# The first layer's preparation with its inverses and key products on VectorE, and the attention's keys and values projected earlier

## The chip, the cores and the metric

The kernel runs on one core of a Trainium2 chip. Its time is the device time in microseconds of one execution. The core has five engines, each with an in-order queue of its own: TensorE (PE; its weight loads are listed as PEld), VectorE (DVE), ScalarE (ACT), GpSimd (POOL) and SyncE (SP), which here starts most of the DMA transfers. The granted TensorE clock is given as a share of the full 2.4 GHz.

## What is computed

The program is a trunk of two layers over 256 context tokens and 512 latent tokens of width 1024, batch 1. The even layer has global attention with normalised queries and keys beside RWKV-7 time mixing in two directions; the odd layer has windowed attention beside a Mamba-2 mixer; each has a squared-ReLU MLP, and a last RMSNorm ends it. The change lies in the preparation of the first layer's time mixing. The part of the reference that this preparation rewrites:

```python
def rwkv7_scan(state0, r, w, k, v, kk, a, reverse):
    def step(S, inp):
        r_t, w_t, k_t, v_t, kk_t, a_t = inp
        sa = jnp.einsum('bhvk,bhk->bhv', S, kk_t)
        S = (S * w_t[:, :, None, :] - sa[..., None] * (kk_t * a_t)[:, :, None, :]
             + v_t[..., None] * k_t[:, :, None, :])
        return S, jnp.einsum('bhvk,bhk->bhv', S, r_t)
...
    kk = (k * k_k).astype(F32).reshape(bsz, T, B_HEADS, HEAD_DIM)
    kk = kk * lax.rsqrt(jnp.sum(kk * kk, axis=-1, keepdims=True) + 1e-12)
    k_dir = k.astype(F32)[:, :, None] * (1.0 + (a - 1.0) * k_a.astype(F32))
```

The kernel does the recurrence in chunks of 32 tokens. For that it needs, for each chunk, head and direction, the inverse of a unit triangular 32x32 matrix made of products of the decayed keys.

## The kernel before, in words

The program is written with a tile scheduler: the source gives the instructions with priorities (`tc.high_priority()`, and `tc.high_priority(-400)` for work that may wait), and the scheduler turns them into one fixed queue for each engine. The order of a queue is thus settled before the program runs, and an instruction that waits holds back everything behind it on its engine.

The stage of interest is in `tile_trunk` and takes from about 100 to 365 us. 768 tokens stand along the free axis, 128 channels (two heads) on the partitions, so the eight heads of the time mixing are four pairs, p = 0 to 3. For each pair the loop does the following:

- `rates(p)`: two small products on TensorE (`lora`, L653) and their tanh on ScalarE (L665).
- `body(p, d)` for both directions d: `kd` on ScalarE (L711) and its product with the keys on GpSimd (L712); `aa` on VectorE (L714); the cumulative sum of the decays on VectorE (L718); the exponentials `e` and `ei` on ScalarE (L723, L724; `ei` has one buffer); the two `ar` products on VectorE (L733, L734); the two `kb` products, one on GpSimd (L735) and one on VectorE (L736); and two transfers that write `ar` and `kb` to memory (L737, L739).
- `load_k`, `load_r` and `load_v` of the next pair: projections on TensorE (L367, three matmuls for each block of weights, since weights and activations are split in two parts, L279 and L280), the token shift on VectorE (L612) and for the keys a norm (sums on TensorE at L623, L381 on VectorE, a power on GpSimd at L382, broadcast at L628 and L631).
- `triangles(p)`: 96 small matmuls `ab` on TensorE (L797), evicted with a mask on VectorE into `abm` (L806). 24 chunks of a pair against 32 in one inverse: three inverses serve the four pairs, and they can begin after pairs 1, 2 and 3.
- `inverse(g)`, g = 0, 1, 2: a transpose on VectorE (L771), two memsets on GpSimd (L773, L774), then 31 pairs of instructions, a multiplication (L778) and a subtraction (L780), each needing the one before, and two transposes back (L781, L782). The results of g = 0 and 1 go to memory through `ttD`, that of g = 2 stays in the tile `lor`. g = 0 and 2 run on VectorE, g = 1 on GpSimd.
- `tail(p)`: the bonus and the gate (L746 to L760).

Behind the loop stand the projections of the attention: `aqk` (keys), `avv` (values) and four queries, each again 48 matmuls of L367, with a norm and a rotation on VectorE (L829 to L831). Then the mixing stage begins: `z` products (L981), and `u` products (L1032), which read all three inverses; their eviction is the first `vu` (L1037). The attention's scores (L1143) run between them. At the other end of the program `to_out` multiplies the normalised latent tokens (L1774) and writes them out.

Of the kernel before, what the change touches and what calls it, by code (L numbers as in the profile page):

```python
# [13 lines left out]
ALU = mybir.AluOpType  # L14
# [4 lines left out]
P = 128  # L19
# [205 lines left out]
def tile_trunk(ctx: ExitStack, tc: tile.TileContext, t: dict, out, cc: Cols, pc: Cols):  # L225
# [303 lines left out]
    with ExitStack() as sa:  # L529
# [140 lines left out]
        def ch(x):  # L670
            return x.rearrange("p (c t) -> p c t", t=C)
# [34 lines left out]
        def body(p, d, kd, mats, sg, a):  # L706

            k, kk, r = ks[p], kks[p], rs_[p]
            A.activation(out=sg, in_=sg, func=AF.Copy, scale=0.5, bias=0.5)
            kd_ = ap.tile([P, NT], F32, tag="kd", name=u("kd"), bufs=2)  # L710
            A.activation(out=kd_, in_=a, func=AF.Identity, scale=kah[:, p:p + 1], bias=kac[:, p:p + 1])  # L711
            G.tensor_tensor(out=kd_, in0=kd_, in1=k, op=ALU.mult)  # L712

# [20 lines left out]
            V.tensor_tensor(out=ar[:, :, 1, :], in0=ch(kk), in1=fa_, op=ALU.mult)  # L734
            G.tensor_tensor(out=kb[:, :, d, :], in0=ch(kd_), in1=fb_, op=ALU.mult)  # L735
            V.scalar_tensor_tensor(out=kb[:, :, 1 - d, :], in0=ch(a), scalar=0.5, in1=fb_, op0=ALU.mult, op1=ALU.mult)  # L736
# [28 lines left out]

        def inverse(g, eng):

            m = lor if g == 2 else aq.tile([P, 1024], F32, tag="im", name=u("im"), bufs=1)
            tmp = aq.tile([P, 256], F32, tag="scan" if g == 2 else "it", name=u("it"), bufs=1)
            m = m.rearrange("p (a b) -> p a b", b=32)  # L770
            V.transpose(m.rearrange("p a b -> p (a b)"), abm[g])  # L771
            n = abm[g]
            G.memset(n, 0.0)  # L773
            G.memset(n.rearrange("p a b -> p (a b)")[:, ::33], 1.0)  # L774
            for s in range(31):
                rows, w = 31 - s, s + 1
                tm = tmp[:, 0:rows * w].rearrange("p (a b) -> p a b", b=w)
                eng.tensor_tensor(out=tm, in0=m[:, s + 1:32, s:s + 1].to_broadcast([P, rows, w]),  # L778
                                in1=n[:, s:s + 1, 0:w].to_broadcast([P, rows, w]), op=ALU.mult)
                eng.tensor_tensor(out=n[:, s + 1:32, 0:w], in0=n[:, s + 1:32, 0:w], in1=tm, op=ALU.subtract)  # L780
            V.transpose(m[0:64].rearrange("p a b -> p (a b)"), n[0:64].rearrange("p a b -> p (a b)"))  # L781
            V.transpose(m[64:128].rearrange("p a b -> p (a b)"), n[64:128].rearrange("p a b -> p b a"))  # L782
            if g < 2:
                nc.sync.dma_start(ttD[g], m.rearrange("p a b -> p (a b)"))

        def triangles(p, mats):
# [22 lines left out]
            for g in range(NCH * p // 32, NCH * (p + 1) // 32):  # L809

                with (ExitStack(), tc.high_priority())[g - 1] if g else tc.high_priority(-400):
                    inverse(g, G if g == 1 else V)
        def attention_qk(n, nm, j):
# [49 lines left out]
        for p in range(4):  # L863
            kd, mats = [], []
            f = rates(p)
            body(p, 0, kd, mats, *f[0])
            if p < 3:
                load_k(p + 1)
            body(p, 1, kd, mats, *f[1])
            triangles(p, mats)  # L870
            if p < 3:
                load_r(p + 1)
            tail(p, kd)
            if p < 3:
                load_v(p + 1)
        for f in (aqk, avv, *q_):
            f()
# [864 lines left out]
    with ExitStack() as se:  # L1742
# [18 lines left out]
        def to_out(s):  # L1761
# [9 lines left out]
            for k in range(0, KT, 2):  # L1771
                xs = xl[:, k:k + 2, ts]
                eng = G if s == LATS[0] and k < 4 else V
                eng.tensor_tensor(out=xs, in0=xs, in1=bc.unsqueeze(1).to_broadcast([P, 2, s[1]]), op=ALU.mult)  # L1774
                nc.sync.dma_start(out[:, k:k + 2, ts], xs)
# [24 lines left out]
```

## Time and profile before

| | |
|---|---|
| Time, median of 3 runs | 2028.16 us (2027.13 to 2031.48) |
| The profiled execution | 2029.69 us, span 2027.9 us |
| Mean granted clock | 0.975 |
| TensorE busy | 1900.6 us, 94% |
| VectorE busy | 1217.1 us, 60% |
| ScalarE busy | 842.6 us, 42% |
| GpSimd busy | 360.6 us, 18% |

The shares are averages over the whole program. The stage of the change is 13% of it, and there the engines stand otherwise: what it is worth is read from stretches of that stage. A group of instructions gives the line, the engine, the operation, what is written and read, and a count behind x. A timeline row has the start and the length in us, and in brackets how long its engine was idle ahead of it and what released it.

### The profile page before, as it was taken

The page shows a single profiled execution, that of the slowest core. Times are in us where ns is not written, and L with a number is a line of the kernel's source. Part 1 is how long each engine was busy: PE and PEld are TensorE (multiplying, and loading weights), DVE is VectorE, ACT ScalarE, POOL GpSimd, SP SyncE. Part 2 cuts the span into 40 slices and gives each one's busy share as a digit, 9 for nine tenths or more (in the row PEclk, how much of TensorE's full clock was granted, in tenths as well). Part 3 has the DMA queues.
Part 4 walks back from the last instruction along what each step waited for, and adds up shares of the span by engine and source line. Part 5 has one row for each costly group of instructions (what it writes and reads, how often), then busy time and mean ns, then how long its engine had stood idle before and what let it go on. Part 6 is the DMA issues. An engine that isn't in the chain of part 4 may idle for free.

```text
span 2027.9 us, 34250 instructions
## 1 busy us (share of the span) xinstructions
PE 1900.6 (94%) x13992; PEld 1547.3 (76%) x13992; DVE 1217.1 (60%) x2070; ACT 842.6 (42%) x1419; POOL 360.6 (18%) x371
## 2 busy tenths in 40 slices
PE   6999868899999899999999999899899799999997
PEld 4776647776765898888888889778668487888886
DVE  5577969575677675555544443865677464344436
ACT  4344432455554443332233224554566444333335
POOL 0022276333222430000000002310153120000002
PEclk9999979899999999999999999999899799999998
DMA  9346554842323643344444432212101133323333
GB/s 333 120 146 193 195 174 143 166 98 59 90 59 110 230 124 93 115 125 135 125 126 131 128 94 73 87 45 73 42 1 43 42 95 97 100 86 102 94 99 109
DMA packets 147885, 228.19 MB, mean 113 GB/s; under 512 B 65024, under 2 KB 102288, under 8 KB 147600
## 3 DMA queue, kind: packets, MB, share of 16 engines
q1 hardware_dynamic: 140912, 213.54, 35.8%
q10 hardware_dynamic: 5456, 7.73, 1.1%
q0 software_dynamic: 1360, 4.73, 0.7%
q8 instruction: 110, 1.80, 0.4%
q14 instruction: 47, 0.39, 0.1%
HBM read 200.00 MB, written 25.96 MB: 111 GB/s over the span
## 4 chain that ended last, share of the span: by engine, by line
PE 69%; DVE 13%; DMA 7%; ACT 4%; issue 4%; POOL 3%; SPq 0%; DVEq 0%; POOLq 0%; ACTq 0%
PE m L367 37%; PE win L367 9%; PE po L341 4%; DMA wmod<-in_wmod_dram 4%; PE pt L332 3%; PE z L981 2%; DVE wlo L280 2%; PE wout L1714 2%; PE wout L1298 2%; PE sc L1143 2%; DMA wraw<-in_win_dram 1%; PE z L1556 1%; DVE junk L1315 1%; PE s L1047 1%; DVE it L778 1%
## 5 line engine op out<-in xcount | busy, mean ns | idle before, releaser
L279 ACT ACTIVATE whi<-wraw 128x1024 fp32r<-128x1024 f32 x214 | 226.4, 1059 | 691.1 <-PE m L367 555.7
L280 DVE TENSOR_TENSOR wlo<-wraw,whi 128x1024 fp32r<-128x1024 f32 x214 | 263.7, 1234 | 204.3 <-ACT whi L279 201.5
L367 PE MATMUL m<-hh,whi 128*128 128x512 f32 (+1 forms) x816 | 239.6, 345 | 3.9 <-ACT relu L1237 2.4
L367 PE MATMUL m<-hh,wlo 128*128 128x512 f32 (+1 forms) x816 | 242.1, 345 | 0.4 <-DVE wlo L280 0.4
L367 PE MATMUL m<-hl,whi 128*128 128x512 f32 (+1 forms) x816 | 241.9, 344 | 0.2 <-POOL hl L503 0.2
L367 PE MATMUL m<-dh,whi 128*128 128x256 f32 (+1 forms) x832 | 238.9, 342 | 2.7 <-DVE xl L1219 2.5
L367 PE MATMUL m<-dl,whi 128*128 128x256 f32 (+1 forms) x832 | 241.1, 341 | 0.0
L367 PE MATMUL m<-dh,wlo 128*128 128x256 f32 (+1 forms) x832 | 240.0, 342 | 0.1
L471 POOL TENSOR_TENSOR acc<-acc,nsq 128x256 f32<-128x256 f32 x42 | 43.6, 1047 | 870.9 <-ACT nsq L470 867.0
L367 PEld LDWEIGHTS m<-dh,whi 128*128 128x128 f32 x832 | 153.4, 188 | 24.9 <-DVE xl L1219 6.2
L367 PEld LDWEIGHTS m<-hh,whi 128*128 128x128 f32 x816 | 152.4, 189 | 23.6 <-ACT relu L1237 2.8
L367 PEld LDWEIGHTS m<-hh,wlo 128*128 128x128 f32 x816 | 153.7, 189 | 20.0 <-DVE wlo L280 0.9
L367 PEld LDWEIGHTS m<-hl,whi 128*128 128x128 f32 x816 | 153.8, 189 | 19.2 <-POOL hl L503 0.4
L367 PEld LDWEIGHTS m<-dl,whi 128*128 128x128 f32 x832 | 154.0, 188 | 18.9
L367 PEld LDWEIGHTS m<-dh,wlo 128*128 128x128 f32 x832 | 153.8, 188 | 18.8 <-DVE wlo L280 0.3
L367 PE MATMUL win<-hl,whi 128*128 128x512 f32 (+1 forms) x512 | 162.2, 350 | 4.7 <-POOL hl L503 3.5
L367 PE MATMUL win<-hh,whi 128*128 128x512 f32 (+1 forms) x512 | 158.0, 355 | 8.6 <-DVE kr L381 5.6
L367 PE MATMUL win<-hh,wlo 128*128 128x512 f32 (+1 forms) x512 | 160.3, 347 | 1.8 <-DVE wlo L280 1.8
L1315 DVE SCALAR_TENSOR_TENSOR junk<-wmod,crow 128x1024 f32<-128x1024 f32 x64 | 78.4, 1225 | 119.0 <-DMA wmod<-in_wmod_dram 118.4
L1219 DVE SCALAR_TENSOR_TENSOR xl<-m,modT,xl 128x512 f32<-128x512 f32 (+1 forms) x144 | 97.3, 686 | 72.2 <-PE m L367 72.2
L367 PEld LDWEIGHTS win<-hh,whi 128*128 128x128 f32 x512 | 95.4, 194 | 31.2 <-issue 12.3
L367 PEld LDWEIGHTS win<-hl,whi 128*128 128x128 f32 x512 | 98.9, 194 | 21.1 <-POOL hl L503 4.7
(416 smaller groups left out, 3624.3 us busy)
## 6 DMA issues: line engine op xcount, KB each, us to landing
wraw<-in_w_dram SPq DMA_DIRECT2D x136, 512.0 KB, 3.6
wmod<-in_wmod_dram SPq DMA_DIRECT2D x96, 512.0 KB, 4.1
wraw<-in_wout_dram SPq DMA_DIRECT2D x40, 512.0 KB, 3.7
wraw<-in_win_dram SPq DMA_DIRECT2D x35, 512.0 KB, 4.0
arD<-ar SPq DMA_DIRECT2D x8, 768.0 KB, 4.2
kbD<-kb SPq DMA_DIRECT2D x8, 768.0 KB, 3.7
ari<-arD SPq DMA_DIRECT2D x24, 256.0 KB, 4.3
kbd<-kbD SPq DMA_DIRECT2D x48, 128.0 KB, 4.0
```

The lines of the kernel that those rows point to most:

```text
L279: A.activation(out=hi, in_=src, func=AF.Copy)
L280: (lo_eng or V).tensor_tensor(out=lo, in0=src, in1=hi.bitcast(F32), op=ALU.subtract)
L332: T.transpose(pt[:, P * j:P * j + P], prob[j][:, P * m:P * m + P], ident)
L341: T.matmul(po[HALVES[i], :], lhsT=vt[:, k_, r], rhs=w_, start=m_ < 2, stop=m_ + 2 >= n, tile_position=(0, 64 * i))
L367: T.matmul(part(ps, s), lhsT=a[:, c], rhs=row(b, k, s), start=first and j == 0 and q == 0, stop=last and j == n - 1 and q == 2)
L471: (V if k == KT - 1 else eng).tensor_tensor(out=at(acc, s), in0=at(acc, s), in1=at(sq, s), op=ALU.add)
L981: T.matmul(ps[:, P * (2 * a + c):P * (2 * a + c) + P], lhsT=kb[:, 2 * m + a, c, :], rhs=ar[:, 2 * m + a, c, :], start=True, stop=True)
L1143: T.matmul(ps[:, cols2(s)], lhsT=qs[:, 2 * j + g, :], rhs=kx[:, g, s[0]:s[0] + s[1]], start=m == 0, stop=m == 1)
L1219: V.scalar_tensor_tensor(out=xs, in0=part(ps, s), scalar=mod(l, which, m, s[2]), in1=xs, op0=ALU.mult, op1=ALU.add)
L1298: T.matmul(part(ps, s), lhsT=a[:, c], rhs=like(b, s), start=k == 0 and q == 0, stop=k == KT - 1 and q == 2)
L1315: V.scalar_tensor_tensor(out=junk, in0=wm, scalar=1.0, in1=crow[:, :, v], op0=ALU.mult, op1=ALU.mult, accum_out=modT[:, l, n, v:v + 1])
L1714: T.matmul(o, lhsT=a[:, c], rhs=b, start=k == 0 and q == 0, stop=k == KT - 1 and q == 2)
```

## The change

Four things change. In `body` the `kd` product (L712) and the `kb` product (L735) go from GpSimd to VectorE, eight instructions each over the four pairs. All three inverses run on VectorE; the second now has the low priority of the first. For the last pair the attention's keys and values are written ahead of `triangles`, no longer behind the loop. In `to_out` the two products that GpSimd did for the first half of the latent tokens go to VectorE.

```diff
-            G.tensor_tensor(out=kd_, in0=kd_, in1=k, op=ALU.mult)
+            V.tensor_tensor(out=kd_, in0=kd_, in1=k, op=ALU.mult)
...
-            G.tensor_tensor(out=kb[:, :, d, :], in0=ch(kd_), in1=fb_, op=ALU.mult)
+            V.tensor_tensor(out=kb[:, :, d, :], in0=ch(kd_), in1=fb_, op=ALU.mult)
...
-        def inverse(g, eng):
+        def inverse(g):
...
-                eng.tensor_tensor(out=tm, in0=m[:, s + 1:32, s:s + 1].to_broadcast([P, rows, w]),
+                V.tensor_tensor(out=tm, in0=m[:, s + 1:32, s:s + 1].to_broadcast([P, rows, w]),
                                 in1=n[:, s:s + 1, 0:w].to_broadcast([P, rows, w]), op=ALU.mult)
-                eng.tensor_tensor(out=n[:, s + 1:32, 0:w], in0=n[:, s + 1:32, 0:w], in1=tm, op=ALU.subtract)
+                V.tensor_tensor(out=n[:, s + 1:32, 0:w], in0=n[:, s + 1:32, 0:w], in1=tm, op=ALU.subtract)
...
-                with (ExitStack(), tc.high_priority())[g - 1] if g else tc.high_priority(-400):
-                    inverse(g, G if g == 1 else V)
+                with tc.high_priority(*((-400,) if g < 2 else ())):
+                    inverse(g)
...
             body(p, 1, kd, mats, *f[1])
+            if p == 3:
+
+                aqk()
+                avv()
             triangles(p, mats)
...
-        for f in (aqk, avv, *q_):
+        for f in q_:
             f()
...
                 eng = G if s == LATS[0] and k < 4 else V
-                eng.tensor_tensor(out=xs, in0=xs, in1=bc.unsqueeze(1).to_broadcast([P, 2, s[1]]), op=ALU.mult)
+                V.tensor_tensor(out=xs, in0=xs, in1=bc.unsqueeze(1).to_broadcast([P, 2, s[1]]), op=ALU.mult)
```

Lines behind the loop stand four higher in the changed kernel (L981 is L985 there, L1037 is L1041). The queues differ at three places that matter here.

TensorE around the last triangles (`ab`). Before, they follow the small products of pair 3 at once, and a projection's rows come behind:

```order
L653 MATMUL lora_2446<-ad_668,lor 128x256
L653 MATMUL lora_2447<-ad_668,lor 128x512
L653 MATMUL lora_2448<-ad_668,lor 128x512
L797 MATMUL ab_2505<-ar_2474,kb_2475 32x32 x16
L797 MATMUL ab_2506<-ar_2474,kb_2475 32x32 x32
L797 MATMUL ab_2505<-kb_2498,ar_2497 32x32 x16
L797 MATMUL ab_2506<-kb_2498,ar_2497 32x32 x32
L750 MATMUL bonus_2675<-kd_2460,cst 128x256
L750 MATMUL bonus_2676<-kd_2460,cst 128x512
L756 MATMUL gate_2683<-gd_675,g2w 128x256
L756 MATMUL gate_2684<-gd_675,g2w 128x512
```

In the changed kernel there stand ahead of them the values' projection, a whole query and half of the next one (`win`, the last of it shown):

```order
L367 MATMUL win_2961<-hh,whi_2965 128x256
L367 MATMUL win_2961<-hl,whi_2965 128x256
L367 MATMUL win_2961<-hh,wlo_2966 128x256
L848 MATMUL vtok_2672<-cst,vraw_2668 128x128 x4
L797 MATMUL ab_2683<-ar_2474,kb_2475 32x32 x16
L797 MATMUL ab_2684<-ar_2474,kb_2475 32x32 x32
L797 MATMUL ab_2683<-kb_2498,ar_2497 32x32 x16
L797 MATMUL ab_2684<-kb_2498,ar_2497 32x32 x32
L750 MATMUL bonus_2853<-kd_2460,cst 128x256
```

The `ab` rows are the same; what stands ahead of them grew by about two projections.

VectorE ahead of the last triangles. Before, the products of pair 3 stand in one piece, without `kd` and `kb` of GpSimd:

```order
L733 TENSOR_TENSOR ar_2474<-fr_2318,e_2467 128x24x32
L734 TENSOR_TENSOR ar_2474<-kk_2046,e_2467 128x24x32
L714 SCALAR_TENSOR_TENSOR aa_2453<-aa_2453,kk_2046 128x768
L736 SCALAR_TENSOR_TENSOR kb_2475<-aa_2453,ei_2468 128x24x32
L714 SCALAR_TENSOR_TENSOR aa_2454<-aa_2454,kk_2046 128x768
L736 SCALAR_TENSOR_TENSOR kb_2498<-aa_2454,e_2490 128x24x32
L746 TENSOR_TENSOR kd_2460<-kd_2460,kd_2483 128x768
L734 TENSOR_TENSOR ar_2497<-kk_2046,ei_2491 128x24x32
L747 SCALAR_TENSOR_TENSOR kd_2460<-kd_2460,par,fr_2318 128x768
L733 TENSOR_TENSOR ar_2497<-fr_2318,ei_2491 128x24x32
```

In the changed kernel the steps of the second inverse (`abm_1654`) and rotations of the attention stand among them, and so do L712 and L735:

```order
L712 TENSOR_TENSOR kd_2460<-kd_2460,fk_2027 128x768
L714 SCALAR_TENSOR_TENSOR aa_2453<-aa_2453,kk_2046 128x768
L778 TENSOR_TENSOR it_2185<-im_2184,abm_1654 128x135
L735 TENSOR_TENSOR kb_2475<-kd_2460,ei_2468 128x24x32
L829 TENSOR_TENSOR rs_2587<-rot_2585,cst 128x512
L830 TENSOR_TENSOR qf_2569<-qf_2569,cst 128x512
L712 TENSOR_TENSOR kd_2483<-kd_2483,fk_2027 128x768
L714 SCALAR_TENSOR_TENSOR aa_2454<-aa_2454,kk_2046 128x768
L736 SCALAR_TENSOR_TENSOR kb_2475<-aa_2453,ei_2468 128x24x32
L780 TENSOR_TENSOR abm_1654<-abm_1654,it_2185 128x27x5
L381 TENSOR_SCALAR rr_2582<-qksum_2575 128x12
L831 TENSOR_TENSOR qf_2569<-qf_2569,rs_2587 128x512
```

Four products moved in for this pair, and steps of an inverse that were not on this engine before.

VectorE ahead of the first `vu`. Before, the third inverse has long ended there:

```order
L987 TENSOR_TENSOR z_3284<-z_3762,cst 128x4x64
L838 TENSOR_SCALAR sq_99<-rr_3206 128x6x2
L987 TENSOR_TENSOR zk_3778<-z_3773,cst 128x256
L987 TENSOR_TENSOR z_3285<-z_3773,cst 128x4x64
L987 TENSOR_TENSOR zk_3787<-z_3782,cst 128x256
L987 TENSOR_TENSOR z_3285<-z_3782,cst 128x4x64
L1037 SCALAR_TENSOR_TENSOR vu_3844<-u_3827,cst,vm_3271 128x256
```

In the changed kernel its last steps (`abm_2182`) and its transposes into `lor` stand right ahead of it:

```order
L778 TENSOR_TENSOR it_2783<-lor,abm_2182 128x60
L780 TENSOR_TENSOR abm_2182<-abm_2182,it_2783 128x2x30
L778 TENSOR_TENSOR it_2783<-lor,abm_2182 128x31
L991 TENSOR_TENSOR zk_3778<-z_3773,cst 128x256
L991 TENSOR_TENSOR z_3285<-z_3773,cst 128x4x64
L780 TENSOR_TENSOR abm_2182<-abm_2182,it_2783 128x31
L991 TENSOR_TENSOR zk_3787<-z_3782,cst 128x256
L991 TENSOR_TENSOR z_3285<-z_3782,cst 128x4x64
L781 STREAM_TRANSPOSE lor<-abm_2182 64x1024
L782 STREAM_TRANSPOSE lor<-abm_2182 64x1024
L1041 SCALAR_TENSOR_TENSOR vu_3844<-u_3827,cst,vm_3271 128x256
```

The third inverse now ends with the row ahead of `vu`, because the steps of the second alternate with its own.

## Rows read from the trace of the kernel before

**Rows 1.** Stretches of the stage: length, busy PE, PEld, DVE, ACT, POOL, granted clock, DMA

```profile
120.00:220.00 100.00, 97.53 (x854) 70.53 (x852) 79.18 (x121) 39.66 (x64) 25.51 (x20) 1.00 0.61 194
220.00:260.00 40.00, 33.88 (x284) 24.66 (x285) 34.60 (x54) 9.67 (x15) 10.74 (x8) 0.91 0.57 191
260.00:300.00 40.00, 23.50 (x339) 13.89 (x338) 28.36 (x31) 14.13 (x26) 31.41 (x38) 0.74 0.53 159
300.00:340.00 40.00, 34.12 (x195) 29.07 (x196) 38.61 (x69) 15.49 (x31) 32.53 (x39) 0.97 0.49 136
340.00:380.00 40.00, 33.61 (x268) 28.24 (x267) 27.58 (x54) 10.75 (x21) 17.42 (x18) 0.88 0.79 181
```

**Rows 2.** Waits from 200 to 300 us: line <- releaser, microseconds, times, longest

```profile
PE ab L797 <- DVE kb L736: 8.3, 1, 8.3
...
PE ab L797 <- DVE ar L734: 7.9, 1, 7.9
...
PE win L367 <- DVE kr L381: 5.6, 1, 5.6
```

**Rows 3.** Timeline ahead of the last triangles: start us, us, engine, line, operation

```profile
284.32 2.51 POOL L712 TENSOR_TENSOR kd<-kd,fk 128x768 f32<-128x768 f32 x1
286.79 1.66 POOL L735 TENSOR_TENSOR kb<-kd,ei 128x768 f32<-128x768 f32 x1
...
289.77 2.42 DVE L734 TENSOR_TENSOR ar<-kk,ei 128x768 f32<-128x768 f32 x1
...
292.24 2.77 PE L797 MATMUL ab<-kb,ar 64*32 64x32 f32 x96 [7.90 <-DVE ar L734]
...
294.70 1.05 DVE L806 TENSOR_TENSOR abm<-ab,cst 128x256 f32<-128x256 f32 x2
```

**Rows 4.** Single operations on the VectorE timeline of the stage

```profile
232.58 0.94 DVE L714 SCALAR_TENSOR_TENSOR aa<-aa,kk 128x768 f32<-128x768 f32 x1
233.45 0.40 DVE L780 TENSOR_TENSOR abm<-abm,it 128x247 f32<-128x247 f32 x1
233.77 0.94 DVE L736 SCALAR_TENSOR_TENSOR kb<-aa,e 128x768 f32<-128x768 f32 x1
...
245.52 0.33 DVE L778 TENSOR_TENSOR it<-im,abm 128x175 f32<-128x175 f32 x1
245.89 0.34 DVE L780 TENSOR_TENSOR abm<-abm,it 128x175 f32<-128x175 f32 x1
...
372.88 0.88 DVE L1037 SCALAR_TENSOR_TENSOR vu<-u,cst,vm 128x256 f32<-128x256 f32 x2 [2.40 <-PE u L1032]
```

**Rows 5.** Groups on GpSimd, 100 to 365 us: xcount | busy us, mean ns | idle

```profile
L778 POOL TENSOR_TENSOR it<-im,abm 128x31 f32<-128x31 f32 (+15 forms) x31 | 20.4, 659 | 2.1
L780 POOL TENSOR_TENSOR abm<-abm,it 128x31 f32<-128x31 f32 (+15 forms) x31 | 20.0, 645 | 2.1
L712 POOL TENSOR_TENSOR kd<-kd,fk 128x768 f32<-128x768 f32 x8 | 18.1, 2262 | 14.6 <-ACT kd L711 14.4
...
L735 POOL TENSOR_TENSOR kb<-kd,e 128x768 f32<-128x768 f32 x4 | 9.0, 2252 | 0.0
L735 POOL TENSOR_TENSOR kb<-kd,ei 128x768 f32<-128x768 f32 x4 | 8.4, 2110 | 0.1
```

**Rows 6.** Groups on VectorE in the same view, 100 to 365 us

```profile
L780 DVE TENSOR_TENSOR abm<-abm,it 128x31 f32<-128x31 f32 (+15 forms) x62 | 27.1, 436 | 1.5
...
L778 DVE TENSOR_TENSOR it<-lor,abm 128x31 f32<-128x31 f32 (+15 forms) x31 | 16.8, 542 | 2.1 <-POOL abm L774 1.3
L714 DVE SCALAR_TENSOR_TENSOR aa<-aa,kk 128x768 f32<-128x768 f32 x8 | 13.9, 1740 | 0.4 <-ACT kd L711 0.4
```

**Rows 7.** One stretch, instructions of L367 alone: length, busy PE, PEld, clock, DMA, GB/s

```profile
299.80:309.40 9.60, 8.87 (x48) 7.38 (x48) 1.00 0.49 117
```

**Rows 8.** Timeline of VectorE at the end of the program

```profile
2013.83 3.44 DVE L1774 TENSOR_TENSOR xl<-xl,rms 128x512 f32<-128x512 f32 x2
...
2021.48 2.48 DVE L1774 TENSOR_TENSOR xl<-xl,nbc 128x512 f32<-128x512 f32 x4 [0.68 <-PE nbc L490]
```

## The prediction

> **What bounds the kernel now.** I read the page first (TensorE is busy 94% of the span), then the stretches of 20 to 100 us for a place where it is not, then the waits inside it, the timeline around those waits, and last the groups of instructions on the two engines between which the change moves work. From 120 to 220 us TensorE is busy 97.5 of 100 us at the full 2.4 GHz, so there is nothing to win while it stays the bound. From 220 to 380 us it is idle 6.1, 16.5, 5.9 and 6.4 us per 40, which is 34.9 us, and the granted clock is 0.91, 0.74, 0.97 and 0.88 there; busy time multiplied by what is missing from 1.0 makes 3.0 + 6.1 + 1.0 + 4.0 = 14 us lost to the lower level of the clock (1.2 GHz) behind the idle places [rows 1]. So 49 us is what a perfect feeding of TensorE would give in this stage, and that is the ceiling of the change.
>
> The reader should see which engine is late. VectorE is busy 34.6 and 38.6 of 40 us on either side of the hole, and GpSimd is busy 31.4 and 32.5 of 40 us from 260 to 340 [rows 1]. Three waits of TensorE make 21.8 us of the idle time: 8.3 and 7.9 us ahead of the two halves of the last triangles, both released by VectorE, and 5.6 us for the key norm of pair 3 [rows 2]. Behind VectorE stands GpSimd: its queue runs kd at 284.32 (2.51 us) and kb at 286.79 (1.66 us) one after the other; VectorE's ar product at 289.77 lies beside the second kb product and takes 2.42 us; the triangles start at 292.24 and are evicted at 294.70 [rows 3]. From there 78.2 us pass to the first vu at 372.88 [rows 3, 4], the point where the mixing stage has its inverse.
>
> **VectorE: what is added and what is given back.** GpSimd loses 20.4 + 20.0 us of the second inverse, 18.1 us of kd and 9.0 + 8.4 us of kb, 75.9 us in all [rows 5]. VectorE gains the 62 steps and the 16 products. A product of this shape (128x768, two operands) takes VectorE 0.94 us with GpSimd idle, and the next instruction starts 0.87 us after it: 16 x 0.87 = 14 us. The mean size of a step is 176 columns (rows times width, averaged over 31 steps); the 128x175 steps take 0.33 and 0.34 us, so 62 x 0.33 = 20.5 us, and start 0.37 us apart where each needs the one before; two independent instructions overlap by 0.07 to 0.08 us, so steps of two inverses that alternate come 0.25 us apart [rows 4]. Added: 14 + 20.5 = 34.5 us of busy time.
>
> Given back is the stretching. The eight L714 products took 13.9 us where 8 x 0.94 would be 7.5; the multiply steps of the third inverse took 16.8 where 31 x 0.33 is 10.2; the 62 subtractions of the first and third took 27.1 where 62 x 0.33 is 20.5 [rows 4, 6]. These three groups alone are 19.6 us over; the ar product of 2.42 us and others of its kind [rows 3] come on top. So VectorE's net is between +15 us (only the three groups come back) and a few us below zero; I take about +5, nearer the second, since every product of two operands beside GpSimd shows the stretch. The point from which the change no longer pays lies near the upper end (rival A).
>
> The Trainium skill, "SBUF — State Buffer", section "SBUF: two separate sides", says that VectorE with two SBUF inputs and GpSimd share a port pair that one of them holds for its whole instruction, while the other is blocked fully. By that rule up to the whole 75.9 us would come back to VectorE, instead of the 20 to 30 that the groups show; the trace bears it out in part only (2.42 us against 0.94, but steps of the inverse of 0.54 against 0.33 us). Against the change stands another page of the Trainium skill, "Perfetto Trace Analysis", section "Optimizing Scalar/DVE Operations": where VectorE is saturated, moving work off it, even to GpSimd, may make sense. VectorE is saturated here, and taken by itself that sentence would make the sum 34.5 us longer on VectorE.
>
> **Up to the last triangles.** The order of TensorE's queue puts the projection of the attention's values and one and a half of its four queries ahead of the last triangles, where they stood behind them: two whole projections net of what was hoisted before. A projection is 48 matmuls, and 48 of them took 8.87 us at the full clock, so 17 us moved [rows 7]. They fill the two waits of 16.2 us. Of these I take 12 back (0 if VectorE is as late as before, 16.2 if the queue hides all), of the 5.6 us 2 (0 to 5.6, since the first inverse still shares the queue), and of the 9 us of slow clock in 220 to 300 us 4 (0 to 9): 18 us. GpSimd's kd and kb behind each other (2.51 + 1.66 + the second kb) fall to products of 0.87 us. So the last triangles are evicted at 294.7 - 18 + 17 = 294 us, as before, but with 17 us of later work done.
>
> **From there to vu.** In VectorE's order 96 steps of two inverses now stand between the eviction and vu, before 62; against that, one query's rotation and two splits of weights have moved ahead. 62 x 0.37 = 23 before, 96 x 0.25 = 24 now: with the rest unchanged VectorE's list is about as long, and before it was stretched by GpSimd over its whole length (VectorE busy 38.6 of 40 us with the subtractions 0.44 on average instead of 0.33) [rows 1, 4, 6]. TensorE has 17 of 78.2 us less to do, which leaves 61. VectorE's share of the stretching there, (542 - 330) ns x 31 + (436 - 330) ns x 62 = 13 us [rows 6], goes as well, so 61 us stands as the later of the two lists with its old waits: vu at 294 + 61 = 355, 17.5 us earlier. Bounds: 78 us again (VectorE just as late: nothing), 46 (TensorE's idle and slow time of this stretch, 12.3 + 5 us, is gone as well, minus 2).
>
> What hides what: the moved projections need splits of weights on ScalarE and VectorE and loads on SyncE's queue; ScalarE is busy 9.7 to 15.5 of 40 us and the DMA engines 0.5 to 0.8 [rows 1], so I cost them at nothing. If that cover is gone, each split on VectorE (1.2 us) stands in the list. The third eviction of pair 2 now stands behind the first inverse's last step and keeps its PSUM bank till then; queued behind it are the scans of pair 3, and TensorE has the attention's keys to do meanwhile.
>
> **The end.** Not in the title of the change: the last normalisation of the first half of the latent tokens gives GpSimd's two products to VectorE. Two took 3.44 us beside GpSimd; four without it take 2.48 [rows 8]. They stand ahead of the last sum of squares, on the path: 3.44 - 2.48 = 1 us gained (0 to 1).
>
> **Sum.** 17.5 + 1 = 18.5 us off the profiled execution (2029.7 us, span 2027.9), which lies 1.5 us above the median of the three runs (2028.16): 2028.2 - 18.5 = 2010.
>
> **Rivals.**
> A, VectorE becomes the bound (slower). One in-order queue now holds the products that release the triangles and 62 more steps that nobody needs soon; products of pair 3 stand among steps of the second inverse, and the last steps of the third with its transposes stand right ahead of vu. If only the three groups' 19.6 us come back of 34.5, VectorE has 15 us more to do in a stretch where it was already busy 38.6 of 40; the covered waits come back as waits for VectorE. Its 11.6 us of idle time from 260 to 300 us [rows 1] take up as much of the 15 as fits there, so vu slips by 4 to 15 us: 2028 + 4 - 1 = 2031 to 2042. It decides from the point where less than some 23 us of stretching goes (34.5 less the 11.6). For it: VectorE's busy share. Against it: the stretch of single operations, 2.42 against 0.94 us.
> B, the gain is eaten downstream (no change). The moved work was TensorE's filling for the late part; without it TensorE waits there for the third inverse, whose steps now alternate with the second's. Then vu comes as before and only 1 us at the end is won: 2025 to 2030.
> C, the port is held fully, so that stretching of 40 us and more goes and the late waits go too: 46 us from eviction to vu instead of 61, or 2010 - 15 = 1995. It is what the rule of the Trainium skill's "SBUF — State Buffer" would give. For it: L714 at 2.5 us. Against it: steps of 0.54 us, which a full block would stretch further.
> D, half: the triangles come earlier but the queries' chain (norm, power on GpSimd, scaling) and the z products with their own waits hold vu to 5 to 12 us of gain: 2016 to 2024.
>
> **Chances.** The forecast (2003 to 2016) 0.50, D 0.16, C 0.11, B 0.11, A 0.12. A measurement of this kernel tells 0.2%, 4 us, from no change. Faster by over 4 us (below 2024): forecast, C and D, 0.77. Slower by over 4 us (above 2032): 0.12. Within: 0.11. The range from 1997 to 2030 leaves out A and most of C, some 0.2.
>
> **What would show it.** Right: in 260 to 300 us TensorE busy over 33 of 40 with a clock near 1.0; L714 and L736 at 0.94 us throughout; the waits of 8.3 and 7.9 us gone; the eviction of the last triangles near 294 and vu near 355; four products of 0.62 us at the end. Wrong: steps of the second inverse on VectorE with TensorE waiting ahead of ab for VectorE again (A), or TensorE's idle time from 330 us on grown by what was saved before (B), or vu released by the transposes of the third inverse at over 365 us. The forecast also falls if any stage behind 380 us moves by more than 2 us, since its order is nearly the same.

## The result, and the profile after

The changed kernel takes 2009.51 us (median of three executions, 2009.04 to 2012.95), the kernel before 2029.82 us beside it: ratio 0.9904, 95% interval 0.988 to 0.9928. A fourth execution of the changed kernel took 3668.61 us, for a reason that no trace here shows; it is left out, though the 2011 us of the expectations below is a median with it in. The profiled execution took 2009.51 us (span 2007.7, mean clock 0.975), 20.2 us less than that of before. The forecast was 2010, within 1997 to 2030. The total was right; the working was right in part only, and by luck two errors in it cancelled.

Where the 20.2 us of span lie is read from three marks in both traces: the first `vu` (L1037, now L1041), the first relu of the MLP (L1237), and the first product of the last normalisation.

| mark | before | after | gained so far |
|---|---|---|---|
| first vu | 372.9 | 363.9 | 9.0 |
| first relu of the MLP | 762.8 | 745.2 | 17.7 |
| last normalisation begins | 2013.8 | 1994.6 | 19.2 |
| last instruction ends | 2024.0 | 2003.8 | 20.2 |

So 9 us were gained in the preparation, where 17.5 were forecast, and 8.7 us in the mixing stage behind it, where nothing was. Another 1.5 us lie in the long stretch behind that, of a size that single executions differ by (below), and 1.0 at the end.

The stretches of the stage in the changed kernel (columns as in rows 1):

```profile
120.00:220.00 100.00, 96.57 (x834) 68.53 (x831) 74.86 (x129) 40.86 (x66) 8.26 (x12) 0.98 0.56 176
220.00:260.00 40.00, 40.00 (x399) 30.52 (x398) 33.79 (x64) 11.18 (x20) 3.35 (x4) 1.00 0.68 216
260.00:300.00 40.00, 34.86 (x311) 22.32 (x310) 33.33 (x61) 16.38 (x26) 9.61 (x4) 0.91 0.71 229
300.00:340.00 40.00, 32.09 (x179) 24.99 (x180) 34.92 (x91) 12.20 (x26) 21.73 (x16) 0.83 0.47 129
340.00:380.00 40.00, 33.87 (x399) 28.65 (x398) 33.61 (x79) 15.18 (x32) 13.00 (x9) 0.87 0.79 187
```

Against rows 1: from 220 to 300 us TensorE's idle time fell from 22.6 to 5.1 us, and its clock rose from 0.91 and 0.74 to 1.00 and 0.91. From 300 to 380 us it is idle 14.0 us, more than the 12.3 before, at a lower clock. GpSimd is nearly empty up to 300 us.

VectorE's groups from 100 to 365 us (count | busy us, mean ns | idle before):

```profile
L780 DVE TENSOR_TENSOR abm<-abm,it 128x31 f32<-128x31 f32 (+15 forms) x93 | 32.9, 366 | 1.3
L778 DVE TENSOR_TENSOR it<-im,abm 128x31 f32<-128x31 f32 (+15 forms) x62 | 21.6, 349 | 0.9
...
L778 DVE TENSOR_TENSOR it<-lor,abm 128x31 f32<-128x31 f32 (+15 forms) x31 | 12.1, 391 | 0.3
...
L712 DVE TENSOR_TENSOR kd<-kd,fk 128x768 f32<-128x768 f32 x8 | 7.7, 957 | 0.5 <-ACT kd L711 0.5
L714 DVE SCALAR_TENSOR_TENSOR aa<-aa,kk 128x768 f32<-128x768 f32 x8 | 7.6, 951 | 0.0
```

L714 takes 951 ns on average and not 1740, L712 costs VectorE 957 ns instead of GpSimd's 2262, and the subtractions average 366 ns instead of 436 [rows 5, 6]. From the start of the program to the first vu, first before, then after (columns as in rows 1):

```profile
0.00:372.80 372.80, 318.54 (x2588) 236.84 (x2588) 268.20 (x443) 135.38 (x231) 120.78 (x133) 0.95 0.59 187
```

```profile
0.00:363.90 363.90, 322.34 (x2588) 236.21 (x2588) 263.42 (x521) 136.24 (x231) 56.03 (x55) 0.96 0.60 192
```

VectorE did 78 instructions more in 4.8 us less of busy time (263.4 against 268.2): more was given back than was added.

TensorE's stretch from the second group's eviction to that of the last triangles, first after, then before (length, busy PE with its count, PEld, DVE, ACT, POOL):

```profile
187.40:302.80 115.40, 108.56 (x1018) 76.54 (x1016) 93.47 (x183) 43.80 (x72) 14.21 (x11) 0.96 0.64 204
```

```profile
189.30:294.70 105.40, 82.79 (x802) 55.87 (x797) 85.58 (x134) 37.09 (x59) 38.41 (x41) 0.88 0.59 189
```

and of these the projections of L367 alone:

```profile
187.40:302.80 115.40, 67.92 (x334) 52.16 (x332) 0.96 0.64 204
```

```profile
189.30:294.70 105.40, 40.42 (x216) 33.40 (x216) 0.88 0.59 189
```

TensorE lost 22.6 us idle there before (105.4 - 82.8) and 6.8 now. But it had 25.8 us more to do, 27.5 of projections and some rotations and sums, less the time that the higher clock saves. So the last triangles are evicted at 303 us, not at 294.7 [rows 3].

VectorE's timeline ahead of the first vu, and at the end of the program:

```profile
360.30 1.23 DVE L781 STREAM_TRANSPOSE lor<-abm 64x1024 f32<-64x1024 f32 x1
361.56 1.93 DVE L782 STREAM_TRANSPOSE lor<-abm 64x1024 f32<-64x1024 f32 x1
363.93 0.88 DVE L1041 SCALAR_TENSOR_TENSOR vu<-u,cst,vm 128x256 f32<-128x256 f32 x2 [0.43 <-PE u L1036]
```

```profile
1994.61 2.49 DVE L1778 TENSOR_TENSOR xl<-xl,rms 128x512 f32<-128x512 f32 x4
...
2001.31 2.48 DVE L1778 TENSOR_TENSOR xl<-xl,nbc 128x512 f32<-128x512 f32 x4 [0.67 <-PE nbc L490]
```

The third inverse's transposes end 0.4 us before vu: VectorE sets this mark now, TensorE before [rows 4]. At the end four products take 2.49 us where two took 3.44 [rows 8].

### The profile page after: what moved, and what is told of

Read it like the earlier page. It is cut to its first block, busy times and chain, and to the rows that moved or that the text cites. A ratio compares the mean times of both kernels' runs of the same rounds, so it can differ in the third digit from the quotient of the medians.

```text
span 2007.7 us, 34218 instructions
## 1 busy us (share of the span) xinstructions
PE 1896.6 (94%) x13992; PEld 1545.1 (77%) x13992; DVE 1215.2 (61%) x2150; ACT 840.7 (42%) x1419; POOL 294.2 (15%) x291
## 4 chain that ended last, share of the span: by engine, by line
PE 77%; DVE 9%; DMA 7%; ACT 3%; issue 3%; POOL 1%; SPq 0%; DVEq 0%; POOLq 0%; ACTq 0%
PE m L367 37%; PE win L367 13%; PE po L341 4%; DMA wmod<-in_wmod_dram 4%; PE pt L332 3%; PE z L985 2%; DVE wlo L280 2%; PE sc L1147 2%; PE wout L1718 1%; PE wout L1302 1%; PE s L1051 1%; PE mod L405 1%; PE lora L653 1%; PE z L1560 1%; DVE junk L1319 1%
## 5 line engine op out<-in xcount | busy, mean ns | idle before, releaser
L367 PE MATMUL m<-hh,whi 128*128 128x512 f32 (+1 forms) x816 | 239.3, 344 | 4.9 <-ACT relu L1241 2.4
L367 PE MATMUL m<-hl,whi 128*128 128x512 f32 (+1 forms) x816 | 241.2, 343 | 0.2 <-POOL hl L503 0.2
L367 PE MATMUL m<-hh,wlo 128*128 128x512 f32 (+1 forms) x816 | 241.3, 344 | 0.0
L367 PE MATMUL m<-dl,whi 128*128 128x256 f32 (+1 forms) x832 | 240.7, 341 | 0.0
L367 PE MATMUL m<-dh,whi 128*128 128x256 f32 (+1 forms) x832 | 238.6, 342 | 1.7 <-DVE xl L1223 1.6
L367 PE MATMUL m<-dh,wlo 128*128 128x256 f32 (+1 forms) x832 | 239.8, 341 | 0.1
L367 PEld LDWEIGHTS m<-dh,whi 128*128 128x128 f32 x832 | 153.3, 188 | 23.9 <-DVE xl L1223 4.9
L367 PEld LDWEIGHTS m<-hh,whi 128*128 128x128 f32 x816 | 152.1, 188 | 24.7 <-ACT relu L1241 2.8
L367 PEld LDWEIGHTS m<-hl,whi 128*128 128x128 f32 x816 | 153.6, 188 | 19.4 <-POOL hl L503 0.4
L367 PEld LDWEIGHTS m<-dl,whi 128*128 128x128 f32 x832 | 153.8, 188 | 19.0
L367 PEld LDWEIGHTS m<-dh,wlo 128*128 128x128 f32 x832 | 153.7, 188 | 18.9 <-DVE wlo L280 0.3
L367 PEld LDWEIGHTS m<-hh,wlo 128*128 128x128 f32 x816 | 153.4, 188 | 19.0 <-DVE wlo L280 0.3
L367 PE MATMUL win<-hl,whi 128*128 128x512 f32 (+1 forms) x512 | 162.3, 348 | 4.7 <-POOL hl L503 3.5
L367 PE MATMUL win<-hh,whi 128*128 128x512 f32 (+1 forms) x512 | 162.3, 362 | 2.7 <-ACT hh L498 2.7
L367 PE MATMUL win<-hh,wlo 128*128 128x512 f32 (+1 forms) x512 | 160.2, 345 | 0.0
L367 PEld LDWEIGHTS win<-hh,whi 128*128 128x128 f32 x512 | 95.4, 194 | 33.6 <-issue 15.7
L367 PEld LDWEIGHTS win<-hl,whi 128*128 128x128 f32 x512 | 98.5, 193 | 22.9 <-issue 5.7
```

The lines of the kernel that those rows point to most:

```text
L367: T.matmul(part(ps, s), lhsT=a[:, c], rhs=row(b, k, s), start=first and j == 0 and q == 0, stop=last and j == n - 1 and q == 2)
```

## The experiments

All compare with the kernel before, run on the same chip. "Behind vu" is the time from the first vu to the MLP's first relu, a stretch with the same 4626 matmuls in every kernel. "Scans" is the start of the last pair's cumulative sums (L718), the first step of that pair's `body` on VectorE.

| kernel | time | ratio (95%) | scans | first vu | behind vu |
|---|---|---|---|---|---|
| before | 2029 | 1 | 271.6 | 372.9 | 389.9 |
| changed | 2009.5 | 0.9904 (0.988 to 0.9928) | 264.3 | 363.9 | 381.3 |
| products alone | 2026.3 | 0.9983 (0.9974 to 0.9992) | 274.5 | 379.9 | 382.4 |
| inverses alone | 2015.2 | 0.9933 (0.9918 to 0.9949) | 262.7 | 357.8 | 389.7 |
| earlier projections alone | 2034.2 | 1.0024 (1.0013 to 1.0034) | 273.8 | 377.2 | 388.4 |
| products and inverses | 2022.4 | 0.9967 (0.9954 to 0.998) | 263.3 | 365.1 | 390.2 |
| inverses, plain priority | 2043.3 | 1.0071 (1.0059 to 1.0084) | 292.5 | 393.7 | 385.7 |
| inverses and earlier projections | 2015.7 | 0.9934 (0.9922 to 0.9946) | 274.2 | 371.1 | 380.3 |
| changed, load on GpSimd | 2020.8 | 0.996 (0.9948 to 0.9973) | 270.3 | 370.7 | 379.5 |
| inverses and kd | 2016.4 | 0.9937 (0.9924 to 0.995) | 262.2 | 358.5 | 392.0 |
| changed, values behind the loop | 2012.9 | 0.992 (0.9905 to 0.9935) | 263.9 | 359.6 | 387.2 |
| inverses, two kd, end | 2010.8 | 0.9908 (0.9893 to 0.9923) | 263.6 | 359.9 | 383.8 |
| the same and two kb | 2007.1 | 0.989 (0.9873 to 0.9906) | 263.2 | 359.1 | 386.3 |
| changed, end undone | 2008.2 | 0.9898 (0.9883 to 0.9913) | 262.3 | 361.6 | 380.2 |

The marks come from one profiled execution each. The last kernel has the queue of the changed one in both stretches, and its marks differ by 2.0, 2.4 and 1.1 us: that is the grain in which the three right columns are to be read.

**Products alone.** On the kernel before:

```diff
-            G.tensor_tensor(out=kd_, in0=kd_, in1=k, op=ALU.mult)
+            V.tensor_tensor(out=kd_, in0=kd_, in1=k, op=ALU.mult)
...
-            G.tensor_tensor(out=kb[:, :, d, :], in0=ch(kd_), in1=fb_, op=ALU.mult)
+            V.tensor_tensor(out=kb[:, :, d, :], in0=ch(kd_), in1=fb_, op=ALU.mult)
```

> One part alone on the kernel before: the 16 kd and kb products on VectorE, the second inverse still on GpSimd. Theory (GpSimd's products stretch VectorE's and hold the last triangles): L714 and L736 fall from 1.7 and 2.1 us towards 1 us, the two waits ahead of the last triangles (8.3 and 7.9 us) fall by half or more, time -5 us (-2 to -9). Rival (only the earlier projections pay): within 2 us of before. Rival (VectorE is the bound, its 14 us of added products count): +5 to +14 us.

2.8 us faster, within the theory's range but not by its mechanism. TensorE's waits from 200 to 385 us:

```profile
PE ab L797 <- DVE kb L736: 13.7, 1, 13.7
...
PE kbc L631 <- DVE tbc L628: 4.0, 1, 4.0
...
PE ab L797 <- DVE ar L734: 3.8, 1, 3.8
```

The two waits ahead of the last triangles went from 16.2 to 17.5 us together. L714 fell to a median of 0.95 us, but VectorE now does four products more for this pair while GpSimd's inverse still runs, and vu comes 7 us later. The gain came behind vu, 7.5 us.

**Inverses alone.**

```diff
-                with (ExitStack(), tc.high_priority())[g - 1] if g else tc.high_priority(-400):
-                    inverse(g, G if g == 1 else V)
+                with tc.high_priority(*((-400,) if g < 2 else ())):
+                    inverse(g, V)
```

> One part alone on the kernel before: all three inverses on VectorE, the products still on GpSimd. Theory: 20.5 us of steps added to VectorE, the stretch of the third inverse's steps (0.54 and 0.44 us against 0.33) goes, 13 us or more; -2 us (-6 to +3). Rival (VectorE is the bound): +8 us, with TensorE waiting for VectorE ahead of ab. Rival (order alone): 0.

13.6 us faster by the ratio, far more than any theory said. Waits from 200 to 360 us:

```profile
PE ab L797 <- DVE kb L736: 4.4, 1, 4.4
...
PE win L367 <- DVE kr L381: 2.3, 1, 2.3
...
PE ab L797 <- DVE ar L734: 1.4, 1, 1.4
```

The three waits of rows 2 fell from 21.8 to 8.1 us, and vu comes 15 us earlier, more than in the whole change. Where these 15 us lie is read from three stretches that end at the last pair's scans, at the eviction of the last triangles and at vu (columns as in rows 1), first before, then this run:

```profile
187.00:271.60 84.60, 78.39 (x741) 52.55 (x740) 67.21 (x122) 28.81 (x46) 16.16 (x22) 0.96 0.65 209
271.60:295.10 23.50, 7.01 (x196) 5.76 (x195) 20.11 (x18) 8.27 (x14) 22.66 (x19) 0.60 0.40 124
295.10:372.90 77.80, 67.98 (x412) 56.00 (x412) 64.91 (x120) 24.29 (x49) 50.95 (x61) 0.92 0.59 159
```

```profile
187.00:262.70 75.70, 73.28 (x732) 51.65 (x730) 66.69 (x121) 28.16 (x46) 13.00 (x12) 1.00 0.63 198
262.70:286.20 23.50, 12.79 (x214) 5.68 (x214) 23.23 (x35) 8.33 (x14) 9.34 (x7) 0.71 0.77 253
286.20:357.80 71.60, 64.56 (x410) 53.35 (x410) 65.70 (x164) 24.16 (x48) 35.55 (x21) 0.95 0.61 170
```

That is 8.9 us ahead of the scans, nothing between the scans and the eviction, and 6.2 us behind it.

The 8.9 us are not the engine's. The edit also takes the second inverse from plain to low priority, and with that TensorE's queue is another from place 1060 of 1805 ahead of the first u: the third pair's triangles stand in the middle of a projection and run at 242 us, where before they stand behind it and run at 256. Their last eviction comes at 257.6 instead of 265.0, ahead of the second inverse's first step in either kernel, before (GpSimd) and here (VectorE):

```profile
267.90 0.25 POOL L778 TENSOR_TENSOR it<-im,abm 128x31 f32<-128x31 f32 x1
```

```profile
264.50 0.18 DVE L778 TENSOR_TENSOR it<-im,abm 128x31 f32<-128x31 f32 x1
```

The runs below bear this out. With the second inverse on VectorE at plain priority (inverses and earlier projections) TensorE's queue is that of before up to the last pair's small products, its first 1406 places, and the scans start at 274.2, as with this inverse on GpSimd (earlier projections alone, 273.8). With low priority they start at 262.2 to 264.3 in eight runs, and at 270.3 in the ninth, which has a load on GpSimd. What the engine itself is worth is read from those two runs at plain priority, whose queues on TensorE differ in 98 of the 1805 places, all behind the small products: vu 6.1 us earlier (371.1 against 377.2), none of it ahead of the scans. No run has the second inverse on GpSimd at low priority.

Between scans and eviction the second inverse did hold GpSimd's own queue in the trace of before (start us, us):

```profile
276.08 1.04 ACT L711 ACTIVATE kd<-aa,kac,kah 128x768 f32<-128x768 f32 x1
...
280.57 2.52 POOL L712 TENSOR_TENSOR kd<-kd,fk 128x768 f32<-128x768 f32 x1
```

ScalarE has delivered the first kd at 277.1; GpSimd takes it up at 280.57, for steps of the inverse run till then. But without that hold the stretch is 23.5 us again: GpSimd's kd and kb still stretch VectorE's products here, and steps of the second inverse now stand among them:

```profile
270.97 2.56 DVE L714 SCALAR_TENSOR_TENSOR aa<-aa,kk 128x768 f32<-128x768 f32 x1
...
275.11 2.42 DVE L736 SCALAR_TENSOR_TENSOR kb<-aa,ei 128x768 f32<-128x768 f32 x1
```

**Earlier projections alone.**

```diff
+            if p == 3:
+                aqk()
+                avv()
             triangles(p, mats)
...
-        for f in (aqk, avv, *q_):
+        for f in q_:
```

> One part alone on the kernel before: keys and values of the attention written ahead of the last triangles, all else as before. Theory: GpSimd's chain still holds the triangles, the projections cover a part of the two waits but stretched VectorE is as late at vu: -4 us (0 to -8). Rival (order alone explains the gain): -15 us or more.

5 us slower: both theories fall. What filled the waits ahead of ab is missing behind the triangles, and vu comes at 377.2. From 250 to 380 us TensorE now waits longest here:

```profile
PE qksum L623 <- ACT sq L820: 10.2, 2, 6.1
```

**Products and inverses together.** The two diffs above.

> Products and inverses on VectorE together, the projections behind the loop as before. Theory (the stretch goes only when GpSimd is empty): more than the sum of the two parts alone, -12 us (-8 to -18). Rival (order alone): within 3 us of before. Rival (VectorE is the bound without the filling): +5 us and more, with TensorE idle ahead of the last triangles.

6.7 us faster, less than the inverses alone. The rival on order looked right here: the projections seemed to bring the other 13 us of the changed kernel. The table tells otherwise: vu is at 365.1 here and at 363.9 there; 9 us of the 13 lie behind vu, where none of the moved work stands.

**Inverses at plain priority**, to have the changed kernel's queue behind vu without the rest (also with the end's products on VectorE); the edit is against the inverses alone:

```diff
-                with tc.high_priority(*((-400,) if g < 2 else ())):
+                with (ExitStack(), ExitStack(), tc.high_priority())[g]:
```

> All inverses on VectorE, the first two at plain priority, the products on GpSimd, no earlier projections; the last normalisation on VectorE too. Its order of TensorE's queue behind the first u is that of the changed kernel, where the run with the inverse alone had the old one. Theory (the mixing stage's order is worth 8 us by itself, and the inverse 14): 2015 - 8 - 1 = 2006 us, with 381 us from the first vu to the first relu of the MLP. Rival (those 8 us came with the products or the earlier projections): 2014 us and 390 us.

14 us slower than before, and vu at 393.7. TensorE's longest wait from 120 to 400 us, and VectorE's timeline ahead of it:

```profile
PE ab L797 <- DVE kb L736: 16.4, 1, 16.4
```

```profile
294.94 1.24 DVE L781 STREAM_TRANSPOSE im<-abm 64x1024 f32<-64x1024 f32 x1
296.19 1.93 DVE L782 STREAM_TRANSPOSE im<-abm 64x1024 f32<-64x1024 f32 x1
298.15 2.83 DVE L718 TENSOR_TENSOR_SCAN sg<-scan,sg 128x256 f32<-128x256 f32 x2
```

This is the mechanism of my rival A, though with the first inverse and not the second: its last steps and transposes stand among the last pair's scans in VectorE's one queue, the scans start at 292.5, and TensorE waits 16.4 us for kb in one piece. In the next run, with only the second inverse at plain priority, the scans start at 274.2, so it is the low priority of the first that keeps most of this away. Behind vu it took 385.7 us, 4 less than the inverses alone; that supports the theory's direction and half of its size. But the changed kernel, from whose TensorE queue there this one differs in 2 of 2711 places, took 381.3: the order alone does not settle this stretch.

**Inverses and earlier projections**, the products back on GpSimd (second inverse at plain priority, the first low).

> The changed kernel with the 16 products back on GpSimd (and the second inverse at plain priority, which gives it the changed kernel's order behind the first u). Theory (the products on VectorE cost more than their stretch gave back once the inverse has left GpSimd): 2011 - 7 = 2004 us. Rival (the prediction's: the products gain): 2014 us or more.

2015.7, as the rival said: vu 7 us later than in the changed kernel, and the same 380 us behind it. But this does not show that the products pay: the scans start 9.9 us later than there, where the priority sets the queue, and from the scans on this run is 2.8 us the faster.

**A load on GpSimd.** The changed kernel with, in `body`, twice:

```diff
+            G.tensor_tensor(out=sg, in0=k, in1=kk, op=ALU.mult)
```

> The changed kernel with 16 more products of 128x768 on GpSimd into a tile that nobody reads: the old load on GpSimd without its dependences. Theory (GpSimd stretches VectorE's products of two operands, and VectorE is the late engine): the products beside it go from 0.95 to 1.7 us and more, VectorE's busy time up by 10 to 20 us, time +5 to +12 us. Rival (the stretch costs nothing, only GpSimd's place in the chain did): within 2 us of the changed kernel's 2011.

About 11 us slower than the changed kernel (2020.8 and 2009.5), vu 6.8 us later with the same queues of TensorE and VectorE up to there. VectorE's groups from 100 to 372 us (lines stand two higher here; L736 is the ar product of kk):

```profile
L714 DVE SCALAR_TENSOR_TENSOR aa<-aa,kk 128x768 f32<-128x768 f32 x8 | 9.2, 1152 | 0.0
...
L736 DVE TENSOR_TENSOR ar<-kk,e 128x768 f32<-128x768 f32 x4 | 7.1, 1767 | 0.0
L736 DVE TENSOR_TENSOR ar<-kk,ei 128x768 f32<-128x768 f32 x4 | 7.0, 1752 | 0.0
```

These ar products take 1.76 us on average where they take 0.95 without GpSimd. Nothing waits for what GpSimd computes here, so this is the price of the shared time alone. The stretch is real, and it costs TensorE.

**Inverses and kd.** The inverses' diff and the first product.

> Inverses and the eight kd products on VectorE, kb on GpSimd, no earlier projections; the order behind the first u is that of the run with the inverse alone, so the two differ in the preparation only. Theory (products cost TensorE's queue some waits, 7 us for 16): +3 us on the inverse alone, 2018. Rival (the prediction's: GpSimd's kd stood ahead of the last triangles, so it gains): 2011.

1.2 us above the inverses alone, vu within 0.7 us: eight products on VectorE cost and gain nothing once the inverse is there. The price of 7 us that I had formed from the products alone falls; so does the prediction's gain.

**The values behind the loop.** The changed kernel, with only the keys earlier:

```diff
                 aqk()
-                avv()
...
-        for f in q_:
+        for f in (avv, *q_):
```

> The changed kernel, but only the keys' projection is written ahead of the last triangles, the values' stays behind the loop. Its queue behind the first u is then the old one (as in the kernel before), with the rest of the change in place. Theory (the queue behind u is worth 9 us and the projections nothing): 2011 + 9 = 2020 us, with 390 us from the first vu to the MLP's first relu against 381. Rival (the changed kernel gains in the preparation, its filling by projections above all): vu later by the values' part, some 4 us, and 381 us behind it: 2015.

2012.9, the same as the changed kernel to within the intervals, but by another way: vu 4.3 us earlier, 387.2 us behind it. So writing the values' projection ahead costs some 2 to 4 us in the preparation, and the stretch behind vu, whose queue changes with it, returns 6.

**Inverses, two kd and the end.** The inverses' diff, the end's, and

```diff
-            G.tensor_tensor(out=kd_, in0=kd_, in1=k, op=ALU.mult)
+            (V if p == 3 else G).tensor_tensor(out=kd_, in0=kd_, in1=k, op=ALU.mult)
```

> The run with the inverse alone, and in addition two kd products (last pair) and the last normalisation on VectorE. TensorE's queue up to the first u is that of the inverse alone but for 16 places, behind it that of the changed kernel. Theory (inverse 14, queue behind u 9, the end 1): vu at 358, 381 us behind it, 2015 - 9 - 1 = 2005 us, below the changed kernel's 2011. Rival (the 9 us belong to the preparations that they were seen with): 2014 us and 390 us.

4.4 us faster than the inverses alone by the medians, with intervals that just touch. The stretch behind vu, first of the inverses alone, then of this kernel (length, busy PE):

```profile
357.80:747.50 389.70, 366.69 (x4626) 287.65 (x4626) 266.74 (x561) 203.15 (x373) 122.92 (x109) 0.99 0.44 113
```

```profile
359.90:743.70 383.80, 364.00 (x4626) 288.64 (x4626) 267.97 (x561) 201.44 (x373) 124.61 (x109) 0.98 0.44 115
```

Ahead of vu TensorE's two queues are alike in all but 16 places; behind it 5.9 us are gone with the same 4626 matmuls: 2.7 of busy time and 3.2 of idle time. The theory's 9 us were too many; this pair gives 6.

**And two kb.** The same edit for the kb product.

> As the run just ahead, with the two kb products of the last pair on VectorE as well: GpSimd has nothing left in front of the last triangles. Theory (what held the last triangles was GpSimd's kd and kb of this pair): waits ahead of ab shorter by 2 to 4 us, 2003. Rival (VectorE in-order is as late as GpSimd): same as the run ahead within 2 us.

2007.1; the last triangles are evicted 1.6 us earlier than without it, vu is 0.8 earlier. The two cannot be told apart, nor this kernel from the changed one (0.989 and 0.9904, intervals overlap). It has the lowest median of all, with 4 products on VectorE instead of 16 and no earlier projections.

**The end undone.**

```diff
-                V.tensor_tensor(out=xs, in0=xs, in1=bc.unsqueeze(1).to_broadcast([P, 2, s[1]]), op=ALU.mult)
+                eng.tensor_tensor(out=xs, in0=xs, in1=bc.unsqueeze(1).to_broadcast([P, 2, s[1]]), op=ALU.mult)
```

> One part of the change undone: two products of the last normalisation on GpSimd again, all else as changed. Theory: 1 us more at the end, nothing else: 2012, the pair of products on VectorE at 1.75 us each beside GpSimd's. Rival (the end is hidden by the last transfer): 2011.

Not slower: 2008.2 against 2009.5. The row did go back, VectorE's and GpSimd's groups of this line:

```profile
L1778 POOL TENSOR_TENSOR xl<-xl,rms x2: 1269/1491/1713, 1994.4 to 1995.7; 128x512 f32<-128x512 f32 x2
L1778 DVE TENSOR_TENSOR xl<-xl,rms x2: 1745/1762/1780, 1994.5 to 1996.2; 128x512 f32<-128x512 f32 x2
```

and from the first such product to the last instruction it is 10.2 us as before, 9.2 in the changed kernel. The 1 us is seen in the rows and is too small for the measured times to show.

## Why the prediction was right, and where its working was not

- **The bound.** TensorE idle for VectorE and GpSimd between 220 and 380 us: right. The waits of 8.3, 7.9 and 5.6 us are gone; 3.0 us are left in front of the last half of the triangles.
- **VectorE's balance.** Predicted +5 us for 78 instructions more; measured up to vu -4.8 (263.4 against 268.2). Against the prediction's own 34.5 us of added work some 39 came back. For the products the stretch went wholly: 951 ns for L714, as predicted; the steps still average 366 and 391 ns where the prediction had 330. That only its three groups would come back, 20 us, was the low bound, rightly not taken. Moving work off VectorE because it is busy, which the prediction set against the change, is answered by the inverses alone: 62 instructions more on VectorE, and vu 15 us earlier.
- **Up to the last triangles.** Here a term was mis-sized. I took two projections, 17 us, as what moved ahead; measured were 118 matmuls of L367 and 27.5 us (67.9 less 40.4), with their sums, broadcasts and transposes 25.8 us net of the clock. The recovery of 18 us was about right (15.8 of idle time, and some clock). 294.7 - 18 + 26 is 303, where it came out.
- **From there to vu.** 61 us predicted, 60.8 measured (303.1 to 363.9), but for another reason: TensorE had 26 us less to do and still needed it, since VectorE's list sets the mark. That is rival B within the preparation: the filling taken early is missing late (TensorE idle 14.0 us from 300 to 380). The projections alone, and the values put back, show it: moved work only moved the idle time, and cost some 4 us up to vu each time.
- **Which part pays.** The prediction gave most of the gain to the filling and to the products. By the runs the inverse alone brings vu forward by 15 us, and the products and the projections together take 6 of these back. The step that failed is that the order of the queues was put at nothing, ahead of the last pair's `body` as well as behind vu. Of the inverse's 15 us, 9 come with the low priority of the second inverse, ahead of the scans, by another order of TensorE's queue; only some 6 are the engine's. In the changed kernel the scans start 7.3 us earlier (264.3 against 271.6), most of its 9 us up to vu. The prediction names the low priority nowhere, and never weighed the second inverse as a part by itself.
- **Behind vu.** "Moves by no more than 2 us, since its order is nearly the same" is false, and by this sign of its own the working fell. The stretch moved by 8.7 us. That the scheduler's queue behind vu falls into three forms was to be seen in the order and was not looked for: eight kernels have the changed kernel's form, or one that differs from it in at most 147 of 2711 places, with 379.5 to 386.3 us, and the six with the old form or a third one 387.2 to 392.0. The pair that differs ahead of vu in 16 places gives 5.9 us. So the form goes with the time in all fourteen kernels, but kernels of one form differ by up to 7 us, and the nearest of the two groups by 1. What in that form saves the time stays open.
- **The end.** 1.0 us, as predicted, read in the rows only.
- **The rivals.** A's mechanism is real (16.4 us of waiting without the first inverse's low priority). C's condition nearly came, with some 39 us of stretching gone where it wanted 40; its time did not, since vu was not at 340. The total of 18.5 was met by 9 + 9, not by 17.5 + 1. Its first term is a slip besides: 293.7 and 61.2 put vu at 354.9, 18.0 us earlier and not 17.5.

The Trainium skill, "SBUF — State Buffer", section "SBUF: two separate sides", would have one engine block the other for its whole instruction. The prediction, and I after it, found that borne out in part only, and that was a misreading of averages. The run with the load bears it out row by row. From its timeline:

```profile
219.04 2.49 POOL L726 TENSOR_TENSOR sg<-fk,kk 128x768 f32<-128x768 f32 x1 [24.25 <-DVE it L780]
```

```profile
219.76 2.59 DVE L736 TENSOR_TENSOR ar<-kk,e 128x768 f32<-128x768 f32 x1
222.27 2.06 DVE L782 TENSOR_TENSOR abm<-abm,it 128x256 f32<-128x256 f32 x1
```

GpSimd's product ends at 221.53, and VectorE's, begun beside it, 0.8 us later. Of the 16 ar products of this run ten took 0.93 to 0.95 us and six 2.17 to 2.59, none between; each of the six ended 0.81 to 0.82 us after the GpSimd product that ran when it began. In the trace of before the same holds for all 19 of VectorE's 40 products of 128x768 up to vu that took over 1.1 us; in the changed kernel none of 56 did. So 1.76 us is an average of blocked and free products. Steps of 0.54 us on average do not speak against it, since the GpSimd steps beside them are short themselves (0.65 us on average [rows 5]).

## What to carry to other kernels

Before crediting a change that moves several things, run each alone, and look for a second change inside each part: here, up to the first vu, one part brought more than the whole and two took some of it back, and most of that part's gain came with a priority that was changed along with the engine. Work that fills a wait must come from somewhere; look at what the same engine does later without it. And where a scheduler writes the queues, compare the whole queue, also behind the place of the edit: a preparation that ends a little differently can leave another order for the next 400 us, and here that stretch moved by as much as the preparation itself.

## What was not expected of the hardware

Two kernels with the same TensorE and VectorE queues up to vu reach it 2.4 us apart, and their medians lie 1.3 us apart with overlapping intervals; differences of that size in single traces are not to be explained. A GpSimd product of 128x768, 1.7 to 2.6 us in the kernel before, took up to 6.77 us in the run with the load, by spans that are rough on this engine:

```profile
127.88 6.77 POOL L726 TENSOR_TENSOR sg<-fk,kk 128x768 f32<-128x768 f32 x1 [0.82 <-ACT ei L724]
```

From 125.92 to 132.94 VectorE ran eight products one behind the other there, each in 0.94 us, and GpSimd's ended 1.7 us after the last of them: GpSimd is held as well.
